# Tie handling of a top-256 selection: sign, square and sums on ACT, one prefix sum and one test on VectorE

## The chip, the cores and the metric

The kernel runs on 1 core of a Trainium2 chip. The metric is the device time of one execution in microseconds (us); lower is better. The core's engines work in parallel, each through its own instruction list in order: PE (TensorE, matrix products), DVE (VectorE), ACT (ScalarE), POOL (GpSimd) and SP (here only the issuer of DMAs; all loads and stores of this kernel stand in SP's one list). An instruction that needs another engine's result waits at the head of its list, and everything behind it waits too.

## The reference, cut to what matters

One layer of a hybrid encoder: a projection of 2048 prompt rows and 128 sample rows, a gated MLP branch, a sparse attention branch, a merge. The change touches the sparse attention's choice of keys:

```python
score = jnp.einsum('bqhl,bqh->bql', rel, wi).astype(jnp.float32) * (N_IDX_HEADS ** -0.5)
score = jnp.where(_chunk_mask(q_pos, k_pos)[None], score, -jnp.inf)
top_val, top_idx = lax.top_k(score, topk)      # topk = 256 (64 for the sample rows)
...
logits = jnp.where(valid[:, :, None, None, :], logits, -jnp.inf)
p = jax.nn.softmax(logits, axis=-1).astype(v.dtype)
```

`lax.top_k` takes, among keys of equal score, those of lowest index first. So a kernel that looks for the 256th largest score as a threshold must still say which of the keys that tie with the threshold are in: the first few, until 256 are reached.

## The kernel before, in words

The rows are cut into 17 tiles of 128 (tile 16 is the sample), the tiles into six groups. Phase A (generator functions `phase_p1` and `phase_p2`, for two halves) is the projection: matrix products with three terms each (line 173), their results copied out by ACT, products and differences formed by DVE and POOL. The last instructions of phase A are those of the gate loop of `phase_p2`: for each of eight weight slices and three groups a gate (ACT, line 479), a product by DVE (line 513) and a store (line 514).

Beside phase A runs the selection, `select(t, lane)`, for tiles 2 to 16, in two lanes that share the engines: tiles 3, 5, ..., 15 in lane 0; 2, 4, 6, 8, 10, 16, 12, 14 in lane 1. For tile t with L = 128(t+1) keys it forms the scores `s` (PE lines 542 and 543, ACT line 545, DVE line 549), then finds the bits of the threshold `cand` one by one: each bit is one pass over L scores, either a count on DVE (line 621) or a sum of signs on ACT (line 631), turn about, then a few instructions on one column. After the last bit come the marks, lines 653 to 673, which the change rewrites: a count of the scores that are at or below the threshold (line 655 by way of line 621), then in chunks of 512 keys an equality test (663), a prefix sum of the ties (664), a copy of the sum's last column (666), a test of the sum against the number of ties still needed (668), and the penalty `pen` (670), 0 for a chosen key and 2^100 for another, stored to DRAM (672). Tile `pen` has one buffer for both lanes; `take("mask")` lets one lane at a time through the marks. There are 39 chunks in the 15 tiles.

Phase B (`phase_b`) is the attention. It begins with the small tiles 0, 1, 2, ...; for each it loads keys (line 703), turns them by PE (706), loads values (712), the penalties (728) and the queries (523 and 524), forms logits (PE 746 and 747, DVE 748), exponentials (ACT 753), turns them (PE 770), splits them (lines 179 and 182), multiplies by the values (787) and copies out (791). Beside it runs the sample's attention (lines 882 to 950, first loads `penx` 896 and `kc` 900), whose buffers take the place of the selection's. Phase C is the merge and the output.

The order on each engine is not that of the source. The source weaves the selection into phase A by estimated costs (the numbers after `yield`), and the framework's scheduler then places each instruction by its own simulation: a selection that is not done when phase A ends stands among the first instructions of phase B.

Of the kernel before, what the change touches and what calls it, by code (L numbers as in the profile page):

```python
# [8 lines left out]
F32 = mybir.dt.float32  # L9
# [3 lines left out]
I8 = mybir.dt.int8  # L13
AF = mybir.ActivationFunctionType
OP = mybir.AluOpType
AX = mybir.AxisListType

P = 128
D = 1024
KD = D // P  # L20
S = 2048
# [7 lines left out]
TOPK = 256  # L29
TOPK_S = LS // 4  # L30
PAD_S = TOPK - TOPK_S
BIG = float(2.0 ** 100)
# [25 lines left out]
def encoder_step(ctx: ExitStack, tc: tile.TileContext, x_prompt, x_sample, cache_k, cache_v, cache_kidx,  # L58
                 norm_g, w_in, ln_g, ln_b, sgu_w, sgu_b, w_pa, w_pb, w_out, final_g,
                 y_prompt, y_sample, o_k, o_v, o_ki, s_k, s_v, s_ki, s_vn):  # L60
    nc = tc.nc
# [36 lines left out]
    perm = ctx.enter_context(tc.tile_pool(name="perm", bufs=1))  # L98
    dram = ctx.enter_context(tc.tile_pool(name="dram", bufs=1, space=bass.MemoryType.DRAM))
    tk = Pool("tk", side="right")  # L100
# [8 lines left out]
    epsr = perm.tile([P, 2], F32, name="epsr")  # L109
    nc.vector.memset(epsr[:, 0:1], RMS_EPS)  # L110
    nc.vector.memset(epsr[:, 1:2], LN_EPS)
    warm = perm.tile([P, 1], F32, name="warm")
    nc.scalar.activation(warm, epsr[:, 0:1], AF.Sqrt)

# [419 lines left out]
    def scores(t):  # L534
        L = (t + 1) * P
        q = q_load(tk, qi_s, t, "qi", eng=BGL)
        hi, lo = pair_of(tk, q, "qih")
        s = tk.tile([P, S], F32, tag="s", name="s", bufs=2)
        for h in range(H):
            for c, n in widths(L):  # L540
                pi = bank("ix")
                nc.tensor.matmul(pi[:, :n], hi[:, h, :], kist[:, c:c + n], start=True, stop=False)  # L542
                nc.tensor.matmul(pi[:, :n], lo[:, h, :], kist[:, c:c + n], start=False, stop=True)  # L543
                r = tk.tile([P, 512], F32, tag="r", name="r", bufs=3)
                nc.scalar.activation(r[:, :n], pi[:, :n], AF.Relu, scale=HD ** -0.5)  # L545
                if h == 0:
                    nc.vector.tensor_scalar(s[:, c:c + n], r[:, :n], wiw[:, t, h:h + 1], None, op0=OP.mult)
                else:
                    nc.vector.scalar_tensor_tensor(s[:, c:c + n], r[:, :n], wiw[:, t, h:h + 1], s[:, c:c + n],  # L549
                                                   op0=OP.mult, op1=OP.add)  # L550
                yield 0.07 + n * 1.04e-3
        nc.vector.memset(s[:HD, L - HD:L], -TOP)
        return s, L
# [41 lines left out]
    def take(*keys):  # L595

        while taken.intersection(keys):
            yield None
        taken.update(keys)

    SIGN_COST = 0.5

    def signs(b, lane, L):
        return b % 2 == lane

    def select(t, lane):

        while GROUP_OF[t][0] not in asked:
            yield 0.5
        keys = ("scores",) if t < NPT else ("scores", "mask")  # L610
        yield from take(*keys)
        s, L = yield from (scores(t) if t < NPT else scores_sample(lane))
        taken.difference_update(keys)
        junk = tk.tile([P, S], I8, tag=f"junk{lane}", name="junk")
        cand = tk.tile([P, 1], I32, tag=f"bc{lane}", name="bc")
        g = tk.tile([P, 1], I32, tag=f"bg{lane}", name="bg")
        cnt = tk.tile([P, 1], F32, tag=f"bn{lane}", name="bn")
        candf = cand.bitcast(F32)

        def count(thr, op):  # L620
            nc.vector.tensor_scalar(junk[:, :L], s[:, :L], thr, 0.0, op0=op, op1=OP.add, accum_out=cnt)  # L621
            return 0.13 + L * 1.04e-3

        yield count(0.0, OP.is_ge)
        nc.vector.tensor_scalar(g, cnt, TOPK - 0.5, -1.0, op0=OP.is_lt, op1=OP.mult)
        nc.vector.tensor_scalar(cand, g, 1 << 30, None, op0=OP.bitwise_xor)
        for b in range(30, -1, -1):
            if signs(b, lane, L):  # L630
                nc.scalar.activation(junk[:, :L], s[:, :L], AF.Sign, bias=candf, scale=-1.0, accum_out=cnt)  # L631
                nc.vector.tensor_scalar(g, cnt, float(L - 2 * TOPK + 1), float(1 << b), op0=OP.is_gt, op1=OP.mult)
                yield SIGN_COST * (0.2 + L * 0.83e-3)
            else:
                yield count(candf, OP.is_ge)
                nc.vector.tensor_scalar(g, cnt, TOPK - 0.5, float(1 << b), op0=OP.is_lt, op1=OP.mult)
            nc.vector.scalar_tensor_tensor(cand, g, (1 << b) >> 1, cand, op0=OP.bitwise_xor, op1=OP.bitwise_xor)  # L637
            yield 0.15

        near = g.bitcast(F32)  # L640
        nxt = tk.tile([P, 1], F32, tag=f"bd{lane}", name="nxt")
        nc.vector.tensor_scalar(g, cand, 0x7fffffff, None, op0=OP.bitwise_and)
        nc.vector.tensor_scalar(nxt, near, float(2.0 ** -126), None, op0=OP.is_ge)
        nc.vector.tensor_tensor(candf, candf, nxt, op=OP.mult)
        nc.vector.tensor_scalar(near, near, float(2.0 ** -24 * (1 + 2.0 ** -20)), None, op0=OP.mult)
        nc.vector.tensor_tensor(nxt, candf, near, op=OP.add)
        yield count(nxt, OP.is_ge)
        nc.vector.scalar_tensor_tensor(near, cnt, TOPK - 0.5, near, op0=OP.is_ge, op1=OP.mult)
        nc.vector.tensor_tensor(candf, candf, near, op=OP.add)
        yield 0.5  # L650

        yield from take("mask")
        need = tk.tile([P, 1], F32, tag=f"bd{lane}", name="bd")
        last = tk.tile([P, 4], F32, tag=f"bl{lane}", name="bl")
        yield count(candf, OP.is_le)
        nc.vector.tensor_scalar(need, cnt, TOPK - L + 0.5, BIG, op0=OP.add, op1=OP.mult)
        n = L if t < NPT else LS
        carry = 0.0
        for c in range(0, n, 512):
            m = min(512, n - c)  # L660
            eq = tk.tile([P, 512], F32, tag="eq", name="eq")
            pre = tk.tile([P, 512], F32, tag="r", name="pre", bufs=3)
            nc.vector.tensor_scalar(eq[:, :m], s[:, c:c + m], candf, BIG, op0=OP.is_equal, op1=OP.mult)
            nc.vector.tensor_tensor_scan(pre[:, :m], eq[:, :m], eq[:, :m], carry, op0=OP.add, op1=OP.bypass)
            carry = last[:, c // 512:c // 512 + 1]
            nc.vector.tensor_copy(carry, pre[:, m - 1:m])
            yield m * 1.5e-3
            nc.vector.scalar_tensor_tensor(eq[:, :m], pre[:, :m], need, eq[:, :m], op0=OP.is_le, op1=OP.mult)
            pen = tk.tile([P, 512], BF, tag="pen", name="pen")
            nc.vector.scalar_tensor_tensor(pen[:, :m], junk[:, c:c + m], BIG, eq[:, :m],  # L670
                                           op0=OP.mult, op1=OP.subtract)
            PS.dma_start(pen_s[t][:, c:c + m], pen[:, :m])
            yield m * 2.1e-3
        taken.discard("mask")

    def select_all_of(ts):
# [424 lines left out]
    def drain(back):  # L1101
        for _ in back or ():
# [8 lines left out]
    hT = first.turn()  # L1111
    nxt = Normed(1, p1, 4, first.gbc)
    back = lanes(chain(select_all_of([0, 1]), *(select(t, 0) for t in (3, 5, 7, 9, 11, 13, 15))),
                 chain(*(select(t, 1) for t in (2, 4, 6, 8, 10, 16, 12, 14))))
    back = weave(phase_p1(0, hT, p1, wa, lambda: nxt.ahead(4)), back, 0.95)
    wa = load_w([cols(C_K), cols(C_KI, 36)], True)
# [73 lines left out]
```

## Time and profile before

| | us |
|---|---|
| median of 3 runs (lowest, highest) | 2210.67 (2208.87, 2212.81) |
| profiled execution, its own time | 2210.12 |
| its span in the trace | 2208.1 |
| PE busy in the span | 2131.6 (97%) |
| DVE busy | 1586.7 (72%) |
| ACT busy | 1217.2 (55%) |
| POOL busy | 591.1 (27%) |

The span begins with the first instruction and ends with the last; what the execution's own time has beyond it is 2.0 us. PE is busy nearly throughout, so a change elsewhere can only act through the few places in which PE waits. In the profile's 40 slices of 55.2 us PE is under nine tenths in the first, the 16th (828 to 883 us), the 26th and 27th (1380 to 1490 us, where it has 6 and 8 tenths) and the last. The end of phase A's last matrix product is at about 1389.2 us in the trace; the dip at 1380 to 1490 us is the start of phase B.

### The profile page before, as it was taken

What the parts mean: (1) busy time and instruction counts of PE and PEld (TensorE: products, weight loads), DVE (VectorE), ACT (ScalarE), POOL (GpSimd) and SP (SyncE); (2) the same over time, 40 slices, a digit from 0 to 9 for tenths busy, and PEclk for the clock granted to TensorE, in tenths of its full rate; (3) what the DMA queues carried; (4) which work ended last, traced back from release to release, by engine and by line L of the source; (5) the groups of instructions that cost most, each with busy time, mean ns of one, the idle gap of its engine ahead of it and who ended that gap; (6) DMA issues with size and microseconds to landing.
All of it is one profiled execution on the core that took longest, in us unless ns stands there. A gap on an engine that the chain in (4) does not pass through costs nothing.

```text
span 2208.1 us, 38238 instructions
## 1 busy us (share of the span) xinstructions
PE 2131.6 (97%) x13896; PEld 2018.2 (91%) x13896; DVE 1586.7 (72%) x4057; ACT 1217.2 (55%) x2181; POOL 591.1 (27%) x693
## 2 busy tenths in 40 slices
PE   8999999999999998999999999689999999999998
PEld 7999999999999998999999999678888999987886
DVE  7128888988987967757876678798887777855443
ACT  6237566656756543446664564677776665743221
POOL 1221122232343221222252221142225443334000
PEclk9999999999999999999999999799999999999999
DMA  6234233122432324121242221444224443054342
GB/s 207 87 106 128 75 108 98 54 72 82 129 109 79 98 70 141 40 70 45 57 134 90 82 66 64 105 112 126 72 64 126 128 127 112 28 158 151 135 153 77
DMA packets 251005, 218.83 MB, mean 99 GB/s; under 512 B 46528, under 2 KB 238656, under 8 KB 250816
## 3 DMA queue, kind: packets, MB, share of 16 engines
q1 hardware_dynamic: 250816, 216.39, 33.3%
q8 instruction: 109, 1.79, 0.3%
q14 instruction: 80, 0.66, 0.1%
HBM read 152.45 MB, written 63.81 MB: 98 GB/s over the span
## 4 chain that ended last, share of the span: by engine, by line
PE 80%; DMA 7%; DVE 6%; ACT 3%; issue 2%; POOL 1%; SPq 1%; ACTq 0%; DVEq 0%; POOLq 0%
PE ps_mm L173 54%; PE ps_po L787 5%; PE ps_tr L770 4%; PE ps_ix L542 3%; PE ps_ix L543 2%; PE ps_mm L746 2%; PE ps_mm L747 2%; PE ps_ix L173 2%; DMA ws<-in_w_in_dram 1%; DVE junk L621 1%; DMA q<-q_s 1%; POOL wl L182 1%; PE ps_mm L798 1%; DMA bl<-bt_s 1%; DMA qi<-qi_s 1%
## 5 line engine op out<-in xcount | busy, mean ns | idle before, releaser
L182 POOL TENSOR_TENSOR wl<-ws,wh 128x256 fp32r<-128x256 f32 (+1 forms) x376 | 303.3, 837 | 923.3 <-ACT wh L179 906.1
L631 ACT ACTIVATE junk<-s,bc 128x384 int8<-128x384 f32 (+14 forms) x232 | 294.2, 1268 | 217.3 <-DVE bc L637 213.6
L173 PE MATMUL ps_mm<-wh,hh 128*128 128x256 f32 (+1 forms) x1360 | 391.5, 289 | 3.1 <-ACT vn L356 2.0
L173 PE MATMUL ps_mm<-wh,hl 128*128 128x256 f32 (+1 forms) x1360 | 392.6, 289 | 0.9 <-DVE hl L182 0.9
L173 PE MATMUL ps_mm<-wl,hh 128*128 128x256 f32 (+1 forms) x1360 | 391.0, 288 | 0.1
L173 PE MATMUL ps_mm<-hh,wh 128*128 128x384 f32 (+1 forms) x1152 | 378.1, 328 | 1.1 <-ACT ev L479 1.1
L173 PE MATMUL ps_mm<-hl,wh 128*128 128x384 f32 (+1 forms) x1152 | 377.4, 328 | 0.0
L173 PE MATMUL ps_mm<-hh,wl 128*128 128x384 f32 (+1 forms) x1152 | 377.1, 328 | 0.0
L621 DVE TENSOR_SCALAR_CACHE_REDUCE junk<-s,bc 128x640 int8<-128x640 f32 (+14 forms) x248 | 351.8, 1421 | 5.3
L173 PEld LDWEIGHTS ps_mm<-wh,hh 128*128 128x128 f32 x1360 | 259.7, 191 | 6.0 <-ACT vn L356 2.2
L173 PEld LDWEIGHTS ps_mm<-wh,hl 128*128 128x128 f32 x1360 | 259.7, 191 | 2.7 <-DVE hl L182 1.2
L173 PEld LDWEIGHTS ps_mm<-wl,hh 128*128 128x128 f32 x1360 | 260.0, 191 | 1.6 <-POOL wl L182 0.3
L549 DVE SCALAR_TENSOR_TENSOR s<-r,wiw,s 128x384 f32<-128x384 f32 (+2 forms) x266 | 201.2, 776 | 61.6 <-ACT r L545 60.9
L173 PEld LDWEIGHTS ps_mm<-hh,wh 128*128 128x128 f32 x1152 | 216.6, 188 | 4.9 <-ACT ev L479 1.5
L173 PEld LDWEIGHTS ps_mm<-hh,wl 128*128 128x128 f32 x1152 | 216.5, 188 | 3.1 <-issue 0.4
L173 PEld LDWEIGHTS ps_mm<-hl,wh 128*128 128x128 f32 x1152 | 216.6, 188 | 2.4
L545 ACT ACTIVATE r<-ps_ix 128x512 f32<-128x512 f32 (+2 forms) x304 | 156.6, 537 | 91.8 <-PE ps_ix L543 78.0
L770 PE MATMUL ps_tr<-ident,sx 128*128 128x128 f32 x1088 | 172.0, 276 | 7.2 <-ACT sx L753 5.7
L182 DVE TENSOR_TENSOR ptl<-ps_tr,pth 128x512 fp32r<-128x512 f32 (+1 forms) x231 | 150.2, 658 | 27.2 <-ACT pth L179 26.1
L179 ACT ACTIVATE pth<-ps_tr 128x512 fp32r<-128x512 f32 (+1 forms) x231 | 128.2, 572 | 74.8 <-PE ps_tr L770 63.3
L787 PE MATMUL ps_po<-pth,vst 128*128 128x256 f32 x544 | 159.8, 309 | 8.2 <-ACT osb L791 6.8
L753 ACT ACTIVATE sx<-sx,mx 128x128 f32<-128x128 f32 (+15 forms) x128 | 153.7, 1202 | 17.4 <-DVE mx L752 17.0
(287 smaller groups left out, 4557.3 us busy)
## 6 DMA issues: line engine op xcount, KB each, us to landing
ws<-in_w_in_dram SPq DMA_DIRECT2D x88, 512.0 KB, 3.9
x<-in_x_prompt_dram SPq DMA_DIRECT2D x41, 512.0 KB, 3.6
q<-q_s SPq DMA_DIRECT2D x34, 256.0 KB, 4.3
out_dram<-x SPq DMA_DIRECT2D x17, 512.0 KB, 2.6
gb_s<-ev SPq DMA_DIRECT2D x40, 192.0 KB, 2.5
ma_s<-ev SPq DMA_DIRECT2D x40, 192.0 KB, 1.9
ma<-ma_s SPq DMA_DIRECT2D x40, 192.0 KB, 3.3
sg<-gb_s SPq DMA_DIRECT2D x40, 192.0 KB, 2.5
```

Source lines behind the costliest of these rows:

```text
L173: nc.tensor.matmul(out, a(k), b(k), start=(n == 0), stop=(n == 3 * nk - 1))
L179: nc.scalar.activation(dst, src, AF.Copy)
L182: (eng or nc.vector).tensor_tensor(dst, src, hi.bitcast(F32), op=OP.subtract)
L542: nc.tensor.matmul(pi[:, :n], hi[:, h, :], kist[:, c:c + n], start=True, stop=False)
L543: nc.tensor.matmul(pi[:, :n], lo[:, h, :], kist[:, c:c + n], start=False, stop=True)
L545: nc.scalar.activation(r[:, :n], pi[:, :n], AF.Relu, scale=HD ** -0.5)
L549: nc.vector.scalar_tensor_tensor(s[:, c:c + n], r[:, :n], wiw[:, t, h:h + 1], s[:, c:c + n], op0=OP.mult, op1=OP.add)
L621: nc.vector.tensor_scalar(junk[:, :L], s[:, :L], thr, 0.0, op0=op, op1=OP.add, accum_out=cnt)
L631: nc.scalar.activation(junk[:, :L], s[:, :L], AF.Sign, bias=candf, scale=-1.0, accum_out=cnt)
L753: nc.scalar.activation(sx, sx, AF.Exp, bias=mx[:, 7:8], scale=HD ** -0.5, accum_out=T.rsum[:, h:h + 1])
L770: nc.tensor.transpose(tv[:, l, hh * P:(hh + 1) * P], pr[hh][:, (l0 + l) * P:(l0 + l + 1) * P], ident)
L787: nc.tensor.matmul(po, vst[:, l0 + l, n, :], pp[:, l, :], start=(l0 + l == 0 and i == 0), stop=(l0 + l == t and i == 1))
```

## The change

Instead of the count, the equality test, the copy and two tests per chunk, ACT now forms over the whole row the sign of `cand - s` (+1 for a score below the threshold, 0 for a tie, -1 above), with its sum, then the square of the sign (0 for a tie, 1 else), with its sum. DVE gets from the two sums the number of ties still needed (`need`), runs a prefix sum over 1 minus the square for each chunk, whose carry is the last column of the chunk before, and one instruction that compares the sum with `need` and adds the sign. That value is above 0 for a key that is not chosen and 0 or less for one that is; ACT's Relu with scale 2^100 makes the penalty of it, in place, and the store follows. The estimated costs after `yield` are changed with it. `SIGN_COST` is 0.5.

```diff
--- before.py
+++ after.py
@@ -109,6 +109,8 @@
     epsr = perm.tile([P, 2], F32, name="epsr")
     nc.vector.memset(epsr[:, 0:1], RMS_EPS)
     nc.vector.memset(epsr[:, 1:2], LN_EPS)
+    one = perm.tile([P, 1], F32, name="one")
+    nc.vector.memset(one, 1.0)
     warm = perm.tile([P, 1], F32, name="warm")
     nc.scalar.activation(warm, epsr[:, 0:1], AF.Sqrt)
 
@@ -649,28 +651,30 @@
         nc.vector.tensor_tensor(candf, candf, near, op=OP.add)
         yield 0.5
 
+
         yield from take("mask")
         need = tk.tile([P, 1], F32, tag=f"bd{lane}", name="bd")
-        last = tk.tile([P, 4], F32, tag=f"bl{lane}", name="bl")
-        yield count(candf, OP.is_le)
-        nc.vector.tensor_scalar(need, cnt, TOPK - L + 0.5, BIG, op0=OP.add, op1=OP.mult)
+        over = tk.tile([P, 2], F32, tag=f"bl{lane}", name="bl")
+        sq = tk.tile([P, S], I8, tag="eq", name="sq")
+        nc.scalar.activation(junk[:, :L], s[:, :L], AF.Sign, bias=candf, scale=-1.0, accum_out=over[:, 0:1])
+        nc.scalar.activation(sq[:, :L], junk[:, :L], AF.Square, accum_out=over[:, 1:2])
+        yield SIGN_COST * (0.4 + L * 1.66e-3)
+        nc.vector.tensor_tensor(need, over[:, 0:1], over[:, 1:2], op=OP.subtract)
+        nc.vector.tensor_scalar(need, need, 0.5, TOPK + 0.5, op0=OP.mult, op1=OP.add)
         n = L if t < NPT else LS
         carry = 0.0
         for c in range(0, n, 512):
             m = min(512, n - c)
-            eq = tk.tile([P, 512], F32, tag="eq", name="eq")
             pre = tk.tile([P, 512], F32, tag="r", name="pre", bufs=3)
-            nc.vector.tensor_scalar(eq[:, :m], s[:, c:c + m], candf, BIG, op0=OP.is_equal, op1=OP.mult)
-            nc.vector.tensor_tensor_scan(pre[:, :m], eq[:, :m], eq[:, :m], carry, op0=OP.add, op1=OP.bypass)
-            carry = last[:, c // 512:c // 512 + 1]
-            nc.vector.tensor_copy(carry, pre[:, m - 1:m])
-            yield m * 1.5e-3
-            nc.vector.scalar_tensor_tensor(eq[:, :m], pre[:, :m], need, eq[:, :m], op0=OP.is_le, op1=OP.mult)
+            nc.vector.tensor_tensor_scan(pre[:, :m], one.to_broadcast([P, m]), sq[:, c:c + m], carry,
+                                         op0=OP.add, op1=OP.subtract)
+            carry = pre[:, m - 1:m]
+            yield m * 2.5e-3
             pen = tk.tile([P, 512], BF, tag="pen", name="pen")
-            nc.vector.scalar_tensor_tensor(pen[:, :m], junk[:, c:c + m], BIG, eq[:, :m],
-                                           op0=OP.mult, op1=OP.subtract)
+            nc.vector.scalar_tensor_tensor(pen[:, :m], pre[:, :m], need, junk[:, c:c + m], op0=OP.is_gt, op1=OP.add)
+            nc.scalar.activation(pen[:, :m], pen[:, :m], AF.Relu, scale=BIG)
             PS.dma_start(pen_s[t][:, c:c + m], pen[:, :m])
-            yield m * 2.1e-3
+            yield m * 1.4e-3
         taken.discard("mask")
 
     def select_all_of(ts):
```

Two places show what the scheduler makes of it. In the changed kernel line numbers are higher by 2 up to the selection and by 4 behind it (kk 703 is 707 there, the store of the penalty 672 is 676, 513 is 515, kst and q 182 are 184, 748 is 752). Prefix sums are listed here as SCALAR_TENSOR_TENSOR with output `pre`; rows with the name ISA are the logits minus penalties of phase B.

SP's list of DMAs around the end of phase A, before: `ma_s` is the last result of phase A, `kk`, `vf`, `pen<-pen_s` and `q` the first loads of phase B.

```order
L514 DMA ma_s_7_105<-ev 128x384
L514 DMA ma_s_7_113<-ev 128x384
L703 DMA kk<-out_dram 128x4x64 x2
L712 DMA vf<-out_dram 128x256
L728 DMA pen<-pen_s_268 128x128
L523 DMA q<-q_s_78 64x8x128
L524 DMA q<-q_s_78 64x8x128
L728 DMA pen<-pen_s_269 128x256
L703 DMA kk<-out_dram 128x4x64 x2
```

The same place in the changed kernel; `pen_s_284<-pen` are the four stores of tile 14's marks, the last of the selection.

```order
L676 DMA pen_s_284<-pen 128x512
L516 DMA ma_s_7_115<-ev 128x384
L707 DMA kk<-out_dram 128x4x64
L676 DMA pen_s_284<-pen 128x512
L707 DMA kk<-out_dram 128x4x64
L716 DMA vf<-out_dram 128x256
L732 DMA pen<-pen_s_270 128x128
L525 DMA q<-q_s_80 64x8x128
L526 DMA q<-q_s_80 64x8x128
L676 DMA pen_s_284<-pen 128x512
L707 DMA kk<-out_dram 128x4x64 x2
```

The four stores stand now between the first loads of phase B (the fourth a few rows further down, between the two halves of tile 1's queries); before they stood among the loads of tiles 5 and 6.

DVE's list at the end of the marks of tile 14, before: `eq`, `pre`, `bl` and `pen` are the marks, all else is phase B.

```order
L663 TENSOR_SCALAR eq<-s,bc 128x384
L182 TENSOR_TENSOR ptl<-ps_tr,pth 128x256
L804 RECIPROCAL rinv<-rsum 128x2
L748 ISA sx,mx<-ps_mm,pen 128x384
L748 ISA mx 128x1
L748 ISA sx,mx<-ps_mm,pen 128x384
L748 ISA mx 128x1
L664 SCALAR_TENSOR_TENSOR pre<-eq,bl 128x384
```

The marks of tile 14 in the changed kernel; `ev` is phase A's last product, `kst` and `q` the first work of phase B.

```order
L669 SCALAR_TENSOR_TENSOR pre<-one,pre,sq 128x512
L674 SCALAR_TENSOR_TENSOR pen<-pre,bd,junk 128x512
L669 SCALAR_TENSOR_TENSOR pre<-one,pre,sq 128x512
L669 SCALAR_TENSOR_TENSOR pre<-one,pre,sq 128x384
L515 TENSOR_TENSOR ev<-ev,ps_mm 128x384
L674 SCALAR_TENSOR_TENSOR pen<-pre,bd,junk 128x512 x2
L184 TENSOR_TENSOR kst<-ps_tr,kst 64x4x128
L674 SCALAR_TENSOR_TENSOR pen<-pre,bd,junk 128x384
L184 TENSOR_TENSOR q<-q,qh 128x1024
```

All tests of the bits and all marks but one stand now ahead of phase B's first instruction on DVE; before 90 of phase B's 640 rows of line 748 stood ahead of the last mark. ACT's list has 17 loads of a function table in either kernel.

## Rows read from the trace of the kernel before

**Rows 1.** The page, span and part 1: busy us, share, instructions of each engine

```profile
span 2208.1 us, 38238 instructions
PE 2131.6 (97%) x13896; PEld 2018.2 (91%) x13896; DVE 1586.7 (72%) x4057; ACT 1217.2 (55%) x2181; POOL 591.1 (27%) x693
```

**Rows 2.** Stretches: start:end, length, busy PE, PEld, DVE, ACT, POOL, PEclk, DMA, GB/s

```profile
core 0: us, PE busy (x) PEld busy (x) DVE busy (x) ACT busy (x) POOL busy (x), PEclk, DMA share, GB/s
1389.20:1400.00 10.80, 1.77 (x8) 1.11 (x7) 6.30 (x14) 6.10 (x8) 0.74 (x1) 0.66 0.67 159
...
1420.00:1440.00 20.00, 17.26 (x109) 15.62 (x107) 18.34 (x56) 15.94 (x47) 7.10 (x9) 0.83 0.42 105
...
sum 110.80, PE 82.12 PEld 72.96 DVE 96.11 ACT 80.44 POOL 33.95; mean PE 13.69 PEld 12.16 DVE 16.02 ACT 13.41 POOL 5.66
...
1500.00:1520.00 20.00, 19.56 (x139) 17.14 (x138) 17.52 (x54) 16.65 (x34) 4.98 (x5) 1.00 0.42 112
```

**Rows 3.** PE's waits from 1389 to 1500 us: total, times, longest

```profile
PE ps_tr L706 <- DMA kk<-out_dram: 9.0, 2, 5.1
PE ps_tr L770 <- ACT sx L753: 5.7, 6, 1.7
PE ps_po L787 <- ACT osb L791: 5.3, 5, 2.2
PE ps_mm L746 <- DVE mx L748: 3.6, 2, 2.7
```

**Rows 4.** PE's waits from 0 to 1389 us, the longest on ACT

```profile
PE ps_mm L173 <- ACT vn L356: 2.0, 1, 2.0
```

**Rows 5.** Groups of the marks on DVE, whole span: busy us, mean ns

```profile
L668 DVE SCALAR_TENSOR_TENSOR eq<-pre,bd,eq 128x512 f32<-128x512 f32 (+4 forms) x39 | 30.6, 784 | 0.0
L664 DVE TENSOR_TENSOR_SCAN pre<-eq,bl 128x512 f32<-128x512 f32 (+3 forms) x24 | 28.2, 1175 | 0.1
L670 DVE SCALAR_TENSOR_TENSOR pen<-junk,eq 128x512 bf16<-128x512 int8 (+4 forms) x39 | 27.4, 704 | 2.0 <-DMA pen_s<-pen 1.8
L621 DVE TENSOR_SCALAR_CACHE_REDUCE junk<-s,nxt 128x384 int8<-128x384 f32 (+14 forms) x15 | 21.4, 1423 | 0.3
L663 DVE TENSOR_SCALAR eq<-s,bc 128x512 f32<-128x512 f32 (+4 forms) x39 | 20.2, 517 | 0.2
L666 DVE COPY bl<-pre 128x1 f32<-128x1 f32 x39 | 5.7, 146 | 0.3
```

**Rows 6.** Groups of the selection on DVE from 1389.2 to 1484 us

```profile
L621 DVE TENSOR_SCALAR_CACHE_REDUCE junk<-s,bc 128x1920 int8<-128x1920 f32 x6 | 13.3, 2209 | 0.1
L668 DVE SCALAR_TENSOR_TENSOR eq<-pre,bd,eq 128x512 f32<-128x512 f32 (+1 forms) x4 | 3.9, 974 | 0.0
```

**Rows 7.** ACT's sign passes, copies of scores (groups), and one table load (timeline)

```profile
L631 ACT ACTIVATE junk<-s,bc 128x384 int8<-128x384 f32 (+14 forms) x232 | 294.2, 1268 | 217.3 <-DVE bc L637 213.6
...
L545 ACT ACTIVATE r<-ps_ix 128x512 f32<-128x512 f32 x160 | 92.4, 590 | 55.0 <-PE ps_ix L543 50.1 <-DVE eq L668 3.7 <-DVE s L549 1.0
L631 ACT ACTIVATE junk<-s,bc 128x1920 int8<-128x1920 f32 x15 | 28.4, 1893 | 24.5 <-DVE bc L637 24.5
...
1408.36 1.28 ACT L753 ACT_TABLE_LOAD   x1
```

**Rows 8.** Timeline of SP and PE at the start of phase B: start, us

```profile
1390.61 1.28 SPq L703 DMA_DIRECT2D kk<-out_dram  x2
1394.60 1.09 PE L706 MATMUL ps_tr<-ident,kk 128*128 128x128 f32 x4 [5.08 <-DMA kk<-out_dram]
1414.85 1.06 PE L706 MATMUL ps_tr<-ident,kk 128*128 128x128 f32 x4
1480.90 0.32 SPq L672 DMA_DIRECT2D pen_s<-pen  x1
```

**Rows 9.** DMA issues: KB each, median us from issue to landing

```profile
kk<-out_dram SPq DMA_DIRECT2D x32, 128.0 KB, 2.8
pen_s<-pen SPq DMA_DIRECT2D x28, 128.0 KB, 1.8
```

## The prediction

> **What bounds the kernel now.** I read the page first: PE is busy for 2131.6 us of 2208.1, so 76.5 us of the span is all that any change off PE could win, plus what PE loses at a low clock [rows 1]. Then I went by stretches of time to find where those 76.5 us lie. Phase A, up to 1389.2 us, has few gaps. The large dip is the start of phase B: of the 110.8 us from 1389.2 to 1500, PE works 82.1, so it idles for 28.7; DVE works 96.1 and ACT 80.4 of the same 110.8, and the granted clock is 0.66 up to 1400 and still 0.83 from 1420 to 1440. From 1500 us on PE is at 19.56 of 20 at full clock, though DVE and ACT do as much per us as before [rows 2]. So phase B can keep PE full with its own work, and something more lies in its first 100 us. The third view, PE's waits in that stretch, names DMA (kk, 9.0 us), ACT's exponentials (5.7) and copies (5.3), and DVE (3.6) [rows 3].
>
> What is in the way there is the selection of tile 14, which is not done when phase A ends: its last store leaves at 1480.9 [rows 8]. DVE's part in the stretch: six counts of 2.21 us of which the first began before 1389.2, so 5 x 2.21 = 11.0; a seventh one of the same length for the final digit, 2.2; four chunks at 517 ns for the equality test, 1.18 for the prefix sum, 146 ns for the copy, 974 ns for the first test and some 0.7 for the second, together 4 x 3.5 = 14.1 [rows 5, 6]. That is 27 us of DVE's 96; ACT has four sign passes of 1.89 in it, 7.6 us [rows 7].
>
> **The change part by part.** Removed from DVE: 15 counts (21.4 us, the row of equal length for the final digit), 39 equality tests (20.2), 39 copies (5.7) and one of two tests per chunk (30.6, the other stays at about 27.4): 78 us of DVE's 1586.7 [rows 1, 5]. The prefix sums stay. Their new form, a constant column and an int8 row, is not in the trace. From below I bound it by the 784 ns of the two-operand test, from above by the longest neighbour, 1.4 us of a count; against 1.18 now that is -15 to +10 us of DVE's work in 39 chunks [rows 5]. I take 0, the nearest row being the prefix sum itself.
>
> Added to ACT: 30 passes over a row (15 signs, 15 squares) at the mean 1.27 us of the sign passes there are, 38 us, and 39 Relus of up to 590 ns, 23 us: 61 us, or 5% more than its 1217 [rows 1, 7]. The square is taken to cost as much as the sign.
>
> *Phase A.* On DVE nothing is won directly: PE waits for it hardly at all there. What the saved work does is move the selection forward. The lists show it: after the change all bits of tile 14 and most of its marks stand ahead of phase B's first DVE instruction. ACT may cost something: its list holds copies that free PE's banks, and a square behind a sign holds it twice as long. The longest wait of PE for ACT in phase A is now 2.0 us, beside 232 sign passes of the same kind [rows 4, 7]. 30 more passes are an eighth more chances; I take +1 us, with 0 and +4 as ends (two such waits more).
>
> *Start of phase B, won.* Of the 28.7 us of idle PE, 9.0 is the wait for the first kk loads, which stays; PE in its even state would idle 2% or 2.5 us [rows 2, 3]. That leaves 17.2 us. The clock gives at most 17% of 17.3 us, 2.9, in the stretch at 0.83; what is lost before 1420 follows phase A's end and stays [rows 2]. So 20 us at most. At least comes back what waits on DVE alone, 3.6 us. Between them I choose by who was crowded: DVE falls from 96 to 69 us of work in the stretch, but ACT only from 80 to 73, and ACT's exponentials and copies are 11.0 us of the named waits [rows 2, 3]. An exponential waits for a maximum from DVE, so some of that is DVE's delay passed on. I take 12 of the 17.2 and 2 for the clock: -14 us, with -4 and -20 as ends.
>
> *Start of phase B, lost.* The four stores of tile 14's marks stand in SP's list between the first loads. The chain of a chunk is: DVE's test 0.70, ACT's Relu 0.59, the issue 0.32, the landing 1.8, and only then the next test, for there is one `pen` buffer: 3.4 us each [rows 5, 7, 8, 9]. The sign and square of tile 14 (2 x 1.89 us) stand about two products of the gate loop before the end. With the first store leaving 1 us after phase A's last product and landing near +3, the second store leaves near +4.6, and the second half of kk behind it; before, both halves were issued in the 1.28 us from 1390.6, so the second left near +2.0 [rows 7, 8]. That is 2.6 us later for the first turn of keys, which came at 1394.6. The other two stores come near +8 and +12, ahead of the loads for tiles 1 and 2; tile 2's turn of keys came at +25.6 (1414.85), so they have room [rows 8]. Price: +3 us, with 0 and +10 (the whole chain in the open) as ends. The sample's first loads move from behind the last store to the third tile as well; they give PE work to fill gaps with, for which I count nothing.
>
> The sum on the profiled execution: 2210.1 + 1 - 14 + 3 = 2200. The median of the runs shown, 2210.67, is half a us above that execution, within their spread, so the forecast for it is the same, 2200.
>
> **A rule that speaks against it.** A table load on ACT takes 1.28 us in this trace [rows 7]. The trace has no square between gelu, silu and sigmoid passes, which fill most of the time in which the selection runs. The Trainium skill (ScalarE: Activation LUTs, section "Table sets: the hidden batching unit") says that functions come in sets of which one is loaded at a time, and that only cheap ones such as relu, copy and abs are in every set; square is not among those that it names. By it each square could force a load and a load back. If that held, 15 x 2 x 1.28 = 38 us more on ACT would come in pieces of 2.6 us beside the copies that PE waits for. The list of the changed kernel speaks against it: 17 table loads, as before. I give it 2 in 100, in the slower rivals.
>
> **Rivals.**
> *Won and given back, within 0.2%.* The exponentials and copies are bound by ACT itself, so that only 4 to 6 us come back; the stores before kk cost 4 and ACT in phase A 1. Time 2209 to 2210. For it: ACT's 80 of 110.8 us hardly shrinks. Against it: after 1500 us ACT is as full, 16.65 of 20, and PE is at 98% [rows 2]. 20 in 100.
>
> *Slower: phase B starts behind the marks.* Before, a late selection only shared DVE with phase B. Now kk, the queries and the sample's buffers stand behind tile 14's four stores, so each us by which the search is late moves the start of phase B. If a wait for ACT in the search, or one for the gate products that stand between its bits in DVE's list, makes the first store leave x us later than I reckon, the time is 2200 + x: slower by 0.2% from x = 15 on. With 20 us, four pairs of a count (2.21) and a sign pass (1.89) with their small steps, it is 2220 [rows 6, 7]. For it: the search is a serial chain and the list is written by a simulation. Against: between two gate products the list of the changed kernel has mostly one such pair, which fits. 10 in 100, with the table rule 12.
>
> **How the numbers follow.** Forecast 2200 with 68 in 100; its own range is 2190 (all 20 us won, nothing lost) to 2206 (8 won, 4 lost). About 0.2%, 4.4 us, is what a measurement of this kernel can tell from no change, so faster means under 2206.3 and slower over 2215.1. Faster 0.68, within 0.2% 0.20, slower 0.12. The range that holds 8 in 10 has to reach into the first rival: 2188 to 2211.
>
> **What would show it.** Right: after the change the sum of ACT's Relu, sign and square passes is near 61 us, DVE's total falls by some 78; the last penalty store leaves within 15 us of phase A's last product; PE's idle time in the 110 us from there is 10 to 18 us instead of 28.7, and the wait on DVE's maxima is gone; the keys of tiles 3 to 5 are turned 8 us or more earlier after phase A's end than before. Wrong: PE's first wait in phase B grows from 5.1 to 10 us or more behind a store of penalties (the slower rival); waits for the exponentials stay at 5.7 us with PE's idle over 22 (the first rival); phase A's last product ends over 4 us after 1389.2 with new waits of PE for ACT (my term for phase A too small).

## The result and the profile after

The changed kernel takes 2196.23 us in the median of four runs (2189.34 to 2197.34; three of them from 2195.6 to 2197.3), the kernel before 2210.37 (2208.87 to 2212.81) beside it. By the medians that is 14.1 us less, where 10 were forecast. The ratio of all runs is 0.9928 with a 95% interval of 0.9909 to 0.9947, which is 15.9 us of 2210, between 11.7 and 20.1; the one run of 2189.34 draws it down. The profiled execution took 2195.58 us, 14.5 less than that of before.

The page, span and busy time of each engine, which answers to [rows 1]:

```profile
span 2193.8 us, 38188 instructions
PE 2126.2 (97%) x13896; PEld 2013.6 (92%) x13896; DVE 1530.8 (70%) x3926; ACT 1271.2 (58%) x2280; POOL 584.8 (27%) x693
```

DVE falls by 56 us and ACT rises by 54. The stretches at the start of phase B, with the columns of [rows 2]; phase A's last product stands at 1388.8 us, so the last line is the same 110.8 us as the sum there. (The times given for the end of phase A, 1389.2 before and 1388.8 here, are those at which its last product starts; it runs for 0.34 us more.)

```profile
1389.10:1400.00 10.90, 1.11 (x5) 0.72 (x4) 4.15 (x7) 2.88 (x5) 0.72 (x1) 0.63 0.64 164
...
1420.00:1440.00 20.00, 17.74 (x97) 14.71 (x97) 14.65 (x50) 13.41 (x39) 4.29 (x6) 0.83 0.68 165
...
1388.81:1499.61 110.80, 94.10 (x594) 80.70 (x593) 80.06 (x291) 79.70 (x213) 31.64 (x42) 0.88 0.62 152
```

PE idles for 110.8 - 94.1 = 16.7 us, 12.0 less than before, and runs 594 products instead of 511. DVE is 16 us less busy, ACT as busy as before. PE's waits in the stretch (total, times, longest), against [rows 3]:

```profile
PE ps_tr L710 <- DMA kk<-out_dram: 6.8, 1, 6.8
PE ps_mm L750 <- ACT qh L181: 5.2, 3, 3.5
PE ps_po L791 <- ACT osb L795: 0.5, 1, 0.5
PE ps_tr L774 <- ACT sx L757: 0.5, 1, 0.5
PE ps_mm L750 <- DVE mx L752: 0.3, 2, 0.2
```

The waits for exponentials, copies and maxima shrink from 14.6 us to 1.3. The wait for kk was two waits before, of 5.08 and 3.95 us, and is one now; a wait for the split queries (`qh`, formed by ACT from the loaded queries) is new. Kk and `qh` together are 12.0 us, for 9.0. Timeline of SP and PE after the change, where [rows 8] stood for before:

```profile
1391.40 0.61 SPq L707 DMA_DIRECT2D kk<-out_dram  x1
1392.31 0.36 SPq L676 DMA_DIRECT2D pen_s<-pen  x1
1392.72 0.57 SPq L707 DMA_DIRECT2D kk<-out_dram  x1
1395.96 1.09 PE L710 MATMUL ps_tr<-ident,kk 128*128 128x128 f32 x4 [6.84 <-DMA kk<-out_dram]
1401.04 0.32 SPq L676 DMA_DIRECT2D pen_s<-pen  x1
1413.53 0.38 PE L912 MATMUL ps_ix<-ident,kc 128*128 128x128 f32 x2
1415.42 0.66 PE L710 MATMUL ps_tr<-ident,kk 128*128 128x128 f32 x4
1422.57 0.60 PE L710 MATMUL ps_tr<-ident,kk 128*128 128x128 f32 x4
1448.37 0.60 PE L710 MATMUL ps_tr<-ident,kk 128*128 128x128 f32 x4
```

The last store of the selection leaves 12.2 us after phase A instead of 91.7. The store at 1392.31 stands between the two halves of kk, and the first wait is 1.8 us longer than the 5.08 of before. But the keys of tiles 2, 3 and 4 (the last three rows) are turned 26.6, 33.8 and 59.6 us after phase A, against 25.65, 37.8 and 59.1 before. The tiles are hardly further on. What is further on is the sample: its first product stands at 1413.53. PE's timeline of before has the same keys of tiles 3 and 4, and the sample's first product, here:

```profile
1427.00 1.09 PE L706 MATMUL ps_tr<-ident,kk 128*128 128x128 f32 x4 [1.40 <-issue]
1448.27 0.60 PE L706 MATMUL ps_tr<-ident,kk 128*128 128x128 f32 x4
...
1493.11 0.44 PE L908 MATMUL ps_ix<-ident,kc 128*128 128x128 f32 x2 [1.74 <-DMA kc<-in_cache_k_dram]
```

The same 110.8 us, with only the instructions that work on the sample's banks (`ps_ix`), first before, then after. The columns are PE, PEld, DVE and ACT, without POOL:

```profile
1389.20:1500.00 110.80, 1.22 (x6) 0.73 (x6) 0.00 (x0) 0.79 (x2) 0.83 0.52 125
```

```profile
1388.81:1499.61 110.80, 21.42 (x86) 13.12 (x86) 6.67 (x21) 5.96 (x18) 0.88 0.62 152
```

So of the 594 products 86 are the sample's, and 508 are the tiles' own, against 511 - 6 = 505 before (in 72.7 us instead of 80.9, in part at a higher granted clock, 0.88 for 0.83). By count, nearly all that PE does more in this stretch is the sample. It is missing later: from the stretch's end to the end of the span, before and after,

```profile
sum 708.10, PE 681.87 PEld 612.10 DVE 459.09 ACT 374.17 POOL 196.74; mean PE 97.41 PEld 87.44 DVE 65.58 ACT 53.45 POOL 28.11
```

```profile
sum 694.19, PE 665.65 PEld 601.65 DVE 455.53 ACT 367.71 POOL 198.24; mean PE 95.09 PEld 85.95 DVE 65.08 ACT 52.53 POOL 28.32
```

PE is busy for 16.2 us less there, at 2.3 us more of idle time. That is the 13.9 us.

Whether the sample's 20 us replaced progress that the tiles would else have made, or made the gain by itself, two profiles can't tell. The experiments were made for that.

### The profile page after: what moved, and what is told of

It is laid out like the page before. It is cut to its first block, busy times and chain, and to the rows that moved or that the text cites. A ratio compares the mean times of both kernels' runs of the same rounds, so it can differ in the third digit from the quotient of the medians.

```text
span 2193.8 us, 38188 instructions
## 1 busy us (share of the span) xinstructions
PE 2126.2 (97%) x13896; PEld 2013.6 (92%) x13896; DVE 1530.8 (70%) x3926; ACT 1271.2 (58%) x2280; POOL 584.8 (27%) x693
## 4 chain that ended last, share of the span: by engine, by line
PE 79%; DMA 6%; DVE 6%; ACT 4%; issue 3%; POOL 2%; SPq 1%; ACTq 0%; DVEq 0%; POOLq 0%
PE ps_mm L175 53%; PE ps_po L791 5%; PE ps_tr L774 4%; PE ps_ix L544 2%; PE ps_ix L545 2%; PE ps_mm L750 2%; PE ps_mm L751 2%; PE ps_ix L175 2%; DMA q<-q_s 2%; DMA ws<-in_w_in_dram 1%; POOL wl L184 1%; PE ps_mm L802 1%; DVE junk L623 1%; DVE bc L639 1%; DMA x<-in_x_prompt_dram 1%
## 5 line engine op out<-in xcount | busy, mean ns | idle before, releaser
L184 POOL TENSOR_TENSOR wl<-ws,wh 128x256 fp32r<-128x256 f32 (+1 forms) x376 | 298.4, 823 | 914.0 <-ACT wh L181 897.3
L623 DVE TENSOR_SCALAR_CACHE_REDUCE junk<-s,bc 128x512 int8<-128x512 f32 (+14 forms) x233 | 331.1, 1422 | 5.6
```

The lines of the kernel that those rows point to most:

```text
L184: (eng or nc.vector).tensor_tensor(dst, src, hi.bitcast(F32), op=OP.subtract)
```

## The experiments

The theory: the gain is the selection leaving the start of phase B, by DVE's work saved. The ratio is to the kernel before on the same chip. The last four columns are from the profiled run: when phase A's last product stands, the time from there to the end of the span, and how long after that product the selection's last store leaves and the sample's first product starts.

| kernel | median us | ratio (95%) | phase A ends | then to the end | last store | sample |
|---|---|---|---|---|---|---|
| before | 2210.37 | 1 | 1389.2 | 818.9 | 91.7 | 103.9 |
| after | 2196.23 | 0.9928 (0.9909 to 0.9947) | 1388.8 | 805.0 | 12.2 | 24.7 |
| e2 | 2211.62 | 1.0015 (1.0003 to 1.0027) | 1391.1 | 824.7 | 62.6 | 74.5 |
| e1 | 2227.11 | 1.0066 (1.0049 to 1.0083) | 1396.8 | 829.5 | 99.9 | 111.9 |
| e3 | 2230.79 | 1.0099 (1.0081 to 1.0117) | 1405.8 | 822.1 | 99.6 | 111.9 |
| e9 | 2214.93 | 1.0024 (1.0010 to 1.0037) | 1389.5 | 822.9 | 85.8 | 95.6 |
| e13 | 2221.35 | 1.0056 (1.0038 to 1.0073) | 1392.7 | 826.7 | 123.6 | 140.9 |
| e5 | 2185.11 | 0.9876 (0.9859 to 0.9893) | 1387.4 | 797.2 | -130.6 | 0.2 |
| e7 | 2198.11 | 0.9938 (0.9921 to 0.9955) | 1389.2 | 805.9 | 19 | 29.1 |
| e6 | 2207.58 | 0.9981 (0.9969 to 0.9993) | 1387.5 | 818.6 | 37.3 | 47.7 |
| e4 | 2204.00 | 0.9977 (0.9965 to 0.9989) | 1389.1 | 813.6 | 12.5 | 95.1 |
| e10 | 2205.81 | 0.9981 (0.9968 to 0.9994) | 1392.5 | 812.9 | 12.3 | 90.7 |
| e11 | 2182.60 | 0.9872 (0.9855 to 0.9888) | 1391.2 | 790.8 | | |
| e12 | 2174.15 | 0.9835 (0.9820 to 0.9850) | 1391.4 | 782.4 | | |

**DVE's work put back (e1, e2, e3).** All on the changed kernel. e1 puts an equality test, a copy and a second test back into each chunk; e2 the count, behind the marks; e3 has both edits.

```diff
@@ e1, before the test of line 674
+            old = sq[:, c:c + m]
+            nc.vector.tensor_scalar(old, s[:, c:c + m], candf, 1.0, op0=OP.is_equal, op1=OP.mult)
+            nc.vector.tensor_copy(cnt, pre[:, m - 1:m])
+            nc.vector.scalar_tensor_tensor(old, pre[:, :m], need, old, op0=OP.is_le, op1=OP.mult)
@@ e2, behind the loop over the chunks
+        nc.vector.tensor_scalar(sq[:, :L], s[:, :L], candf, 0.0, op0=OP.is_le, op1=OP.add, accum_out=cnt)
```

> The changed kernel with the work of the chunks alone put back on VectorE (per chunk an equality test, a copy of a column, a test of two operands, about 57 us in all), results not used. 45 of phase B's logit instructions stand ahead of the last mark, as in the kernel before. Theory: nearly all of the gain is lost, 2205 to 2212. Rival (the gain goes in proportion to the work removed, wherever it lies): 57 of 78 us back, so 2206; the two part by where the last mark stands, not by the time.

> The changed kernel with one count of a whole row put back on VectorE per tile (15 counts, about 21 us in all), after the tile's marks; its result isn't used. Its list has 24 of phase B's logit instructions ahead of the last mark (45 before the change, 0 after it). Theory (crowded start of phase B): the time follows how much of the selection lies in phase B, so about half of the 14 us are lost again: 2201 to 2206. Rival 1 (the order is luck of the scheduler, the amount of work doesn't matter): anything from 2194 to 2212, no relation to the three others. Rival 2 (the early sample attention fills gaps): its list has the sample's first matrix product at place 143 of phase B (283 before, 40 after), so also about half.

> The changed kernel with all the VectorE work put back that the change removed, as instructions whose results aren't used: a count per tile, and per chunk an equality test, a copy of one column and a test of two operands. ACT's new work stays. 47 of phase B's logit instructions stand ahead of the last mark. Theory: back to the time before the change, 2208 to 2213, with PE idle for 26 us or more of the 110.8 us behind phase A's last product; a little more is possible as ACT's 60 us stay. Rival (the gain came from the new order of the sums, signs on ACT, fewer waits in the marks): stays under 2203.

All three took more time than the theory had. e2, with 21 of the some 78 us, already has none of the gain: the last store moves back to +62.6, the sample's start to +74.5 (its profiled run, 2217.6, lies 6 us above its median, so one of its columns, phase A or the rest, is too high). The step from work to time is not linear, and e2's time lies inside what its rival 1, the luck of the order, allows. e1 and e3 are slower than the kernel before, and part of that is phase A, 8 and 17 us longer than in the changed kernel. e3's stretch at the start of phase B, with the columns of [rows 2]:

```profile
1405.79:1516.59 110.80, 82.13 (x467) 72.44 (x466) 98.25 (x308) 85.47 (x195) 33.75 (x43) 0.77 0.49 117
```

and PE's waits for ACT's copies of scores in its phase A:

```profile
PE ps_ix L544 <- ACT r L547: 8.6, 15, 1.5
```

DVE's 98 us in the stretch are near those of the kernel before; but the kernel carries ACT's new passes too, and the 8.6 us of waits for ACT were 1.8 before. So ACT's passes, which I had at +1, had to be priced by themselves.

**ACT's passes alone (e13).** On the kernel before, behind its marks, a sign and a square for each tile, whose results nothing uses:

```diff
+        nc.scalar.activation(junk[:, :L], s[:, :L], AF.Sign, bias=candf, scale=-1.0, accum_out=last[:, 0:1])
+        nc.scalar.activation(junk[:, :L], junk[:, :L], AF.Square, accum_out=last[:, 1:2])
         taken.discard("mask")
```

> The kernel before with ACT's 30 whole-row passes (sign and square, with their sums, about 42 us) added behind each tile's marks, for nothing: no instruction of VectorE waits for them but the next use of the buffer. With all of VectorE's old work beside all of ACT's new work the changed kernel came to 2231, 20 us over the kernel before. Theory (ACT has room, that loss came from the marks' chain of VectorE and ACT): 2209 to 2214. Rival (ACT's load itself costs time in phase A when VectorE isn't relieved): 2217 to 2226.

It is the rival's result, 10 us slower, though not by the rival's phase A alone: 3.5 us lie there and 7.8 behind it. Its groups of passes on ACT (busy us, mean ns):

```profile
L674 ACT ACTIVATE junk<-s,bc 128x384 int8<-128x384 f32 (+14 forms) x15 | 19.0, 1265 | 12.8 <-DVE pen L670 12.8
L675 ACT ACTIVATE junk<-junk 128x384 int8<-128x384 int8 (+14 forms) x15 | 17.5, 1168 | 0.1
```

Its stretch at the start of phase B:

```profile
1392.67:1503.47 110.80, 79.17 (x465) 68.35 (x463) 95.33 (x299) 79.66 (x186) 30.41 (x34) 0.82 0.42 103
```

and on SP's timeline the last store of the selection:

```profile
1516.27 0.33 SPq L672 DMA_DIRECT2D pen_s<-pen  x1
```

With 36.5 us of passes the selection ends 32 us later after phase A (+123.6 for +91.7), as a serial chain would in which they stand. PE idles for 31.6 us in the stretch instead of 28.7, and runs 465 products for 511. In the change the same passes take DVE's place in that chain, so I read their price as part of its net gain; it is no term that could be left at +1 whatever DVE saves.

**The cost estimates alone (e9).** The kernel before with the changed numbers after `yield`.

```diff
-        yield count(candf, OP.is_le)
+        count(candf, OP.is_le)
+        yield SIGN_COST * (0.4 + L * 1.66e-3)
...
-            yield m * 1.5e-3
+            yield m * 2.5e-3
...
-            yield m * 2.1e-3
+            yield m * 1.4e-3
```

> The kernel before, with the estimated costs of the changed kernel between the instructions of the marks and nothing else changed. 40 of phase B's logit instructions stand ahead of the last mark. Theory: 2207 to 2212, as before. Rival (the new estimates, not the work, move the selection): 2195 to 2203.

5 us slower, 3 above the theory's range, with the last store at +85.8: the new estimates alone don't move the selection out. But they change the order, and that alone cost 5 us here.

**A shorter selection (e5).** The changed kernel with 24 of 31 bits, which leaves out the seven lowest bits of the threshold.

```diff
-        for b in range(30, -1, -1):
+        for b in range(30, 6, -1):
```

> The changed kernel with 24 of the 31 bits of the threshold searched, so other keys are chosen: about 105 passes over rows fewer, 140 us of work on VectorE and ACT together. No store of marks stands behind phase B's first load. Theory: nothing more is won on VectorE and ACT, only the wait for the first keys falls back from 6.8 to about 5 us and the selection's last stores leave the list: 2189 to 2195. Rival (work taken off VectorE and ACT pays wherever it lies, 14 us for 78 less 61): 2165 to 2182.

4 us below the theory's range and 3 above the rival's. The selection ends 130.6 us before phase A does, the sample's first product stands at its very end, and the stretch reads

```profile
1387.43:1498.23 110.80, 98.57 (x639) 84.86 (x637) 81.32 (x304) 84.70 (x226) 32.53 (x36) 0.94 0.54 131
```

so 12.2 us of idle PE are left, for 16.7. In the profiled runs phase A is 1.4 us shorter than in the changed kernel and what follows it 7.8.

**The stores (e6, e7).** e6 issues the penalty stores from ACT's list, so that they don't stand before kk in SP's. e7 gives `pen` a second buffer (at two other places too, not shown; `one` moves into a column of `epsr`, to make room).

```diff
@@ e6
-            PS.dma_start(pen_s[t][:, c:c + m], pen[:, :m])
+            nc.scalar.dma_start(pen_s[t][:, c:c + m], pen[:, :m])
@@ e7
-            pen = tk.tile([P, 512], BF, tag="pen", name="pen")
+            pen = tk.tile([P, 512], BF, tag="pen", name="pen", bufs=2)
```

> The changed kernel with the stores of the penalties issued from ACT's list, behind the Relu, instead of SP's. Theory (the four stores in SP's list cost about 2 to 3 us at the start of phase B): 2192 to 2197, with PE's first wait for keys at about 5 us instead of 6.8; but its list has 16 of phase B's logit instructions ahead of the last mark, which may take as much back. Rival (the wait has another cause): the first wait stays at 6.8 us and the time at 2196.

> The changed kernel with two buffers for the penalties instead of one (and the column of ones kept in another tile for room). Theory: VectorE's waits for the store of the last chunk, 10.2 us in all, are gone, the last store of the selection leaves some 5 us earlier after phase A's end, and the time is 2192 to 2196. Rival (those waits have cover): 2195 to 2198, no difference.

e6's first wait is what was expected, but it took 11 us more than the changed kernel. PE's waits in its first 111 us of phase B:

```profile
PE ps_tr L710 <- DMA kk<-out_dram: 4.8, 1, 4.8
PE ps_mm L750 <- DVE mx L752: 4.7, 3, 2.6
```

The scheduler had put 16 of phase B's logit rows ahead of DVE's last mark, the last store went to +37.3 and the waits for maxima were back. It therefore says little on the stores. It does show that the saved work is not enough by itself: e6 has all of it (with the 39 issues more in ACT's list), starts its sample 56 us earlier than the kernel before, and takes as long after phase A (818.6 for 818.9 us).

In e7 DVE no longer waits for stores (10.2 us in the changed kernel), but the last store leaves 7 us later, not 5 earlier, and the time is the changed kernel's, the rival's result. Its stretch at the start of phase B:

```profile
1389.15:1499.95 110.80, 86.65 (x573) 74.77 (x572) 83.08 (x291) 82.53 (x214) 33.13 (x43) 0.91 0.63 149
```

PE is idle there for 24.2 us, not 16.7, in a kernel that is as fast, and 79 of the 573 products are the sample's, so the tiles have 494, fewer than the 505 of before. PE's busy time in this stretch, at a mean granted clock of 0.91 here and 0.88 in the changed kernel, is therefore no measure of the gain by itself.

**The sample held back (e4, e10).** The changed kernel, in which the sample's attention waits for the row sums of tile 5: in e4 its loads wait for them, in e10 the loads go early and only the products wait. Both hold it until some 91 to 95 us after phase A, near where it stood before.

```diff
@@ both: row sums of tile 5 kept, start of attend_sample
+            if T.t == 5 and not begun:
+                begun.append(T.rsum[:, h:h + 1])
...
+        while not begun:
+            yield 0.5
@@ e4, ahead of the loads
+            if b < 2:
+                nc.gpsimd.tensor_copy(kc[:, 0, 0:1], begun[0])
@@ e10, behind the loads
+            if b < 2:
+                nc.vector.scalar_tensor_tensor(kc[:, 0, 0:1], begun[0], 0.0, kc[:, 0, 0:1], op0=OP.mult, op1=OP.add)
```

> The changed kernel, with the sample's attention held back until tile 5 of phase B has its first row sums, by a copy of one column into its key buffers: its first matrix product stands at place 288 of phase B, as before the change (283), instead of 40. The selection is over ahead of phase B as in the changed kernel. Theory (VectorE and ACT freed of the selection are the gain): 2195 to 2199. Rival (the gain is that the sample's matrix products fill PE's gaps in the first 50 us): 2203 to 2210.

> The changed kernel, with the sample's key loads issued as early as in it, but its products held back (place 277 of phase B, before the change 283, in the changed kernel 40) by one small VectorE instruction on each of the first two key buffers, which adds 0 times a row sum of tile 5. Held back in the run before this one at its loads, the sample's attention cost 5 to 8 us, but SP's list stood behind that hold for 6.4 us. Theory (relieved VectorE and ACT are the gain): 2195 to 2200. Rival (the sample's products in PE's gaps are half of it or more): 2202 to 2208.

Both are the rival's results, 2204.0 and 2205.8: with the last store where the change has it, less than half of the gain is left (5.9 and 5.6 us of 14.1 by the medians). e4 blocks SP's list for 6.4 us besides, e10 doesn't, and the two agree. e10's stretch, first whole, then `ps_ix` alone:

```profile
1392.50:1503.30 110.80, 86.04 (x589) 77.46 (x587) 83.00 (x293) 83.31 (x211) 37.59 (x48) 0.91 0.59 142
```

```profile
1392.50:1503.30 110.80, 4.13 (x19) 2.92 (x19) 0.43 (x1) 1.31 (x4) 0.91 0.59 142
```

Here the tiles do get on: 589 - 19 = 570 products of theirs, for 505 before and 508 in the changed kernel. So I read that the room which DVE gives up is used by whoever is ready. PE still idles for 24.8 us. Its waits there, against the 5.3, 5.7 and 3.6 us of [rows 3]:

```profile
PE ps_po L793 <- ACT osb L797: 4.3, 2, 2.9
PE ps_tr L776 <- ACT sx L757: 3.3, 3, 2.5
PE ps_mm L750 <- DVE mx L752: 2.5, 1, 2.5
```

With the selection out of the way but the sample late, 10.1 of the 14.6 us are there again. In e4 the copies (osb) and exponentials are 4.2 and 2.7 us.

**Without the sample (e11, e12).** Before and after, each without the loop of the sample's attention; its output then comes from the gate alone.

```diff
-        q = q_load(bp, q_s, NPT, "q", eng=BGL)
...
-        for b in range(DB):
...
-        BGL.dma_start(b, bo_s)
...
+        BGL.dma_start(b, zb_s[NPT])
```

> The kernel before, with the sample's attention left out (its loads, products and softmax; its output is made of the gate alone). Taken with the next kernel: theory (relieved engines): the two differ by 11 to 15 us, as with the sample. Rival (early sample work): they differ by 3 to 7 us.

> The changed kernel, with the sample's attention left out in the same way. Theory: 11 to 15 us under the kernel before without the sample. Rival: 3 to 7 us under it.

2182.60 (2181.41 to 2183.72) and 2174.15 (2172.51 to 2175.58): 8.5 us apart, between the two theories. The stretches of e11 and of e12:

```profile
1391.15:1501.95 110.80, 79.96 (x503) 69.96 (x502) 97.40 (x311) 79.21 (x191) 31.68 (x35) 0.85 0.49 124
```

```profile
1391.40:1502.20 110.80, 87.60 (x561) 79.50 (x560) 78.12 (x273) 83.38 (x210) 48.19 (x51) 0.86 0.59 154
```

The idle time of PE falls by 7.6 us (30.8 to 23.2), and the rest of the run is 8.4 us shorter. But these kernels still form the sample's output from the gate, and its products (`ps_ix`) move forward too; first e11, then e12:

```profile
1391.15:1501.95 110.80, 0.66 (x4) 0.42 (x4) 0.00 (x0) 0.58 (x1) 0.85 0.49 124
```

```profile
1391.40:1502.20 110.80, 6.59 (x28) 4.94 (x28) 1.10 (x2) 0.57 (x1) 0.86 0.59 154
```

So 5.9 of the 7.6 us are that output; the tiles have 533 products for 499 and 1.7 us more of busy time. The 8.5 us are at most the tiles' part.

Together: of the 15.9 us that the ratio 0.9928 is, the tiles' own relief gives 4 to 5 (e10 and e4 by their ratios, 0.0019 and 0.0023 of 2210) to 8.5 at most (without the sample), and the sample's earlier start, by subtraction, the other 7 to 12; by the medians, 14.1 us in all, each part is 5.6 to 8.5. The intervals, the two gates' own cost, and an order that is new in each list (5 us in e9) don't allow a finer split.

## Why the prediction was right, and which terms were not

**The place held, the mechanism in part.** Phase A's end moved by 0.4 us and what follows is 13.9 us shorter. The last store leaves within 15 us of phase A, PE's idle time fell to 16.7, inside the 10 to 18, and the wait on DVE's maxima is gone (3.6 to 0.3). Of these signs the idle time is the weakest: e7 is as fast with 24.2 us of it.

**Start of B won, -14.** Measured 13.9 net, where this term and the stores together were -11. That the size is near is luck: two errors oppose each other. The step that failed is that the sample's move was counted at nothing. Its buffers take the selection's place: in each kernel of the table that holds nothing back and whose selection outlasts phase A, its first product starts 10 to 17 us behind the selection's last store, wherever that is. With its products held late, e4 and e10 lose more than half of the gain. And the tiles' own part, for which I had all 14, is only 4 to 8.5. My test for it failed as well: the keys of tiles 3 to 5 were to be turned 8 us or more earlier, and tile 3's came 4.0 earlier, tile 4's 0.5 later, tile 5's 1.1 earlier. The 9.0 us for kk, which I took to stay, were two waits, of which the second went and one for the queries came.

**Who was crowded.** I read DVE's delay into the waits for exponentials and copies, and in the changed kernel they fell from 11.0 to 1.0 us with ACT as busy as before. But that doesn't rule out the first rival, in which ACT itself binds them and 4 to 6 us come back. With DVE relieved and the sample held late, 7.6 (e10) and 6.9 us (e4) of these waits are there and the gain is 5.6 and 5.9 us, near the 4 to 6 that this rival has coming back. The wait for copies hardly changed: 4.3 and 4.2 us for 5.3, and without the sample 4.8 (e12) for 6.6 (e11). So I now read part of what vanished as covered by the sample's products, not relieved; that rival's 2209 to 2210 missed by the sample's move, which it left out as well.

**Lost to the stores, +3.** Measured +1.8 in the first wait, in the place and by the store that the text named; e6 without it has 4.8. What that costs in the end is not shown: the first logit product stands 11.8 us after phase A's last product before the change and 11.7 after it.

```profile
1400.99 0.87 PE L746 MATMUL ps_mm<-kst,qh 128*128 128x128 f32 x3 [0.27 <-DVE kst L182]
```

```profile
1400.50 0.90 PE L750 MATMUL ps_mm<-kst,qh 128*128 128x128 f32 x3 [3.45 <-ACT qh L181]
```

**ACT in phase A, +1.** In the changed kernel PE's waits for ACT did rise, in phase A (compare [rows 4]):

```profile
PE ps_ix L544 <- ACT r L547: 4.4, 5, 1.5
PE ps_mm L175 <- ACT hh L181: 3.9, 2, 3.5
```

while other waits went; before had this one, which after lacks:

```profile
PE ps_tr L252 <- DVE bg L636: 2.5, 1, 2.5
```

Up to its end PE idles for 22.4 us of phase A instead of 21.6, and the end still came 0.4 us sooner, as its products were busy for 1.2 us less (1366.4 for 1367.6). So the term came out within its range, but its reasoning was too narrow: e13 shows that the passes, without DVE's saving, cost 10 us (in the profiled runs 11, of which 3.5 in phase A and the rest behind it).

**DVE's and ACT's work.** The groups that answer to [rows 5] and [rows 7]:

```profile
L674 DVE SCALAR_TENSOR_TENSOR pen<-pre,bd,junk 128x512 bf16<-128x512 f32 (+4 forms) x39 | 31.3, 802 | 10.4 <-DMA pen_s<-pen 10.2
L669 DVE TENSOR_TENSOR_SCAN pre<-one,pre,sq 128x512 f32<-128x512 f32 (+3 forms) x24 | 29.7, 1236 | 0.1
L662 DVE TENSOR_TENSOR bd<-bl 128x1 f32<-128x1 f32 x15 | 2.4, 160 | 14.0 <-ACT sq L660 14.0
```

```profile
L675 ACT ACTIVATE pen<-pen 128x512 bf16<-128x512 bf16 (+4 forms) x39 | 22.3, 572 | 40.8 <-DVE pen L674 34.8 <-issue 2.4 <-DVE bc L639 1.8
L659 ACT ACTIVATE junk<-s,bc 128x384 int8<-128x384 f32 (+14 forms) x15 | 18.9, 1262 | 5.9 <-DVE bc L651 5.8
L660 ACT ACTIVATE sq<-junk 128x384 int8<-128x384 int8 (+14 forms) x15 | 17.5, 1170 | 0.7 <-PE ps_ix L589 0.4
```

The prefix sum with its new operands costs nearly what it did (1236 ns for 1175; with the 15 first chunks, which form a group of their own, 2.6 us more in all), as taken. The test that stays costs 802 ns, not 704, and the subtraction for `need` 2.4 us. By the sum of all groups DVE has 71 us less (1777.8 to 1706.5), for 78; the page's 56 is less, since busy time counts once where two records overlap. ACT's three new groups are 58.7 us, for 61. The square costs slightly less than the sign, and the trace has 17 table loads as before, none of it at line 660. So the rule weighed at 2 in 100, of the Trainium skill (ScalarE: Activation LUTs, "Table sets: the hidden batching unit"), had nothing to act on here.

**Slower: B behind the marks.** It did not come; the first store left 0.2 us after phase A's last product. Its price of 1 us for each us was not tested: in e2 the last store leaves 50 us later than in the changed kernel, but the first keys are turned 5.0 us after phase A, earlier than in the changed kernel (7.2), so its loads don't stand behind the stores.

**What stays open.** Why e1 and e3 have a longer phase A was not taken apart further than the waits for ACT's copies. The split between relief and sample stays as wide as above. Nor is the luck of the order ruled out as a part of the gain: e9 shows that a new order of the lists alone can cost 5 us, e2 loses all of the gain with most of the saved work in place, and why e6, which has all of it, its last store at +37.3 and its sample at +47.7, has nothing of the gain behind phase A is not known. Among the kernels with the sample only e5 was faster than the changed kernel, and it leaves bits out.

## What to carry to other kernels

Where a serial side job ends late, ask what stands behind its buffers as well as what it crowds: the work that those buffers admit early may be worth more than the relief. Count products by owner in the dip before and after, since that tells who filled it, but hold a gain read there against a second kernel of the same time, as e7 is here. Price passes that are moved to an idle engine by their place in the chain, not by that engine's busy share. A change of order from one edited line can cost as much as the edit is worth, so read the place of the last mark before the time of an experiment is believed.

## What the runs showed that was not expected

Holding back a second, independent stream (the sample) for some 66 to 70 us cost more than half of the gain, though the selection was out of the way. Two kernels of the same time (the changed one and e7) differ by 7.5 us in PE's idle time at the place where the gain was looked for. And 36.5 us of passes on an engine that was busy for 55% of the span cost 10 us of time, with the end of the chain in which they stood 32 us later.
